# First column group of the second FFN's input projection: two separate projections replaced by one paired group, two of its eight weight pairs by Strassen's scheme

## The chip, the core and the metric

The kernel runs on one core of a Trainium2 chip. The metric is the device time of one launch in microseconds (us). The kernel before was run three times.

## What is computed

The reference is one block of a streaming encoder on 256 frames of width 2048: a feed-forward network (FFN), a mixer with two kinds of attention, cross attention to 256 memory tokens, and a second FFN. Each of the four adds its input times 2^(1/4) and ends in a layer norm. Cut to the part around the change:

```python
def swiglu_ffn(x, w_in, w_out):
    g, u = jnp.split(x @ w_in, 2, axis=-1)
    return (jax.nn.silu(g) * u) @ w_out
...
h = layer_norm(ALPHA * h + xa, ln_x_g[l], ln_x_b[l])
h = layer_norm(ALPHA * h + 0.5 * swiglu_ffn(h, ffn2_w_in[l], ffn2_w_out[l]), ln_ffn2_g[l], ln_ffn2_b[l])
```

Here `x` is 256 x 2048, `w_in` 2048 x 11008 (5504 gate columns, then 5504 up columns) and `w_out` 5504 x 2048, all float32.

## The kernel before

**Numbers.** Every operand of a matmul is kept as two parts, `hi` (the value in the matmul's reduced float32 format) and `lo` (the rest). A product takes three matmuls: x_hi w_hi, x_lo w_hi and x_hi w_lo. A megabyte of weights (128 partitions x 2048 values) is loaded by SyncE (SP) into one of three `raw` tiles; ScalarE (ACT) makes `hi` by two casts of 1024 columns (L264) and VectorE (DVE) makes `lo` by one subtraction (L267). The activations are normalised, turned and split in the same way.

**Tiles.** The contraction of 2048 is 16 steps of 128, called `kt` 0 to 15. The 256 tokens are two halves of 128, `tt` 0 and 1. The activations stand in four tiles T0 to T3 of four `kt` each. A matmul (128 x 128 by 128 x 512) adds into a PSUM bank of 128 tokens x 512 columns; there are eight banks, four named `mm` and four named `at`.

**Column groups.** An FFN's input projection is done in groups of 512 up columns and 512 gate columns. An ordinary group is a *pair group* (`pair_group`, L646): it walks over eight weight pairs, each of two `kt`, 512 up and 512 gate columns, and adds into four banks, one for each token half and each of up and gate. A *plain* pair costs 2 x 2 x 2 x 3 = 24 matmuls (`mm_pair`, L303, matmul at L311). Some pairs are done by Strassen's scheme (`mm_sums`, L347, matmul at L366): the 2 x 2 x 2 block product is made from seven products instead of eight, so 21 matmuls. This needs sums of weight blocks (`weight_sums`: L248 once and L250 twice on DVE, into a tile of 2048 columns, then two casts at L264 into X2 and one subtraction at L267 into X3), sums of activation blocks (`forms_step`, `sum_forms`: L321, four times L325, then a split at L255 and L256), four more banks `qs`, and `shared` (L679 to L684), which turns the four banks into four addends. Where a group has such addends, `hidden` (L716) adds them to the banks (L725, L726) ahead of silu and product.

**The first group of the second FFN** is another kind, `first_group` (L687), since its activations come from the layer norm just ahead of it. It has weight arrays of its own, `ffn2_gate` and `ffn2_up`, of which each megabyte holds four `kt` and 512 columns. Gate comes first: its four loads are all kept, and `skewed` (L813) runs them for token half 0 and then again for token half 1 (`mm_tok`, L298, 12 matmuls a part). Load j reads tile Tj. The kept weights stand in both `hi`/`lo` units and in X0/X1 and H4/H5. Up follows, four loads, each for both halves (24 matmuls a load). In all 8 x 12 + 4 x 24 = 192 matmuls. After each of the last three up loads one `forms_step` is recorded, since the next group needs the forms of pairs 2, 4 and 6.

**The layer norm beside it.** The last part of the cross attention's output projection (`w_xo_r`) is skewed too: token half 0 is finished 48 matmuls before token half 1. In those 48 matmuls DVE finishes the statistics of half 0 (L752, L390, L395), forms 1/sqrt by three Newton steps (L400, L375, then L378 and L379 three times), and the shift `nb` (L403). Then DVE scales quarters 0 and 2 of the row (L413) and ACT quarters 1 and 3 (L415); TensorE (PE) turns each quarter by four transposes against the identity (L421); ACT (L428) and DVE (L430) apply gain and bias, two 128-column blocks each; ACT casts the `hi` part (L255) and DVE subtracts the `lo` part (L256) of tile T0, T1, T2 or T3. The same steps for half 1 are the three pieces `before` that `first_group` weaves into its gate parts.

**What sets the order.** All work is recorded as a list of items with weights (`add`, `weave`); `run` (L179) walks the list, and loads weights ahead of the item that needs them, as far as the two units allow. When it loads an item's weights it also makes the weight sums of the next item in the queue, if that one is a Strassen pair (`form_sums(i + 1)`). A scheduler then puts the instructions of each engine in one fixed order; each engine runs its own list strictly in that order and waits at semaphores.

Of the kernel before, what the change touches and what calls it, by code (L numbers as in the profile page):

```python
# [22 lines left out]
D_FF = 5504  # L23
# [4 lines left out]
SUMS_IN = {2: ("X0", 0), 4: ("X0", 1), 6: None}  # L28
# [13 lines left out]
SUM_HOME = ("X2", "X3"),  # L42
# [59 lines left out]
class Kernel:  # L102
# [197 lines left out]
                        start=(start and j + wi + xi == 0), stop=(stop and j == n - 1 and wi == 1),  # L300
                    )

    def mm_pair(self, ps, w, n, x, kts, first, last):  # L303

        for wi in range(2):
            for j, kt in enumerate(kts):
                for tt in range(2):
                    for g in range(2):
                        c = (2 * j + g) * n
                        for xi in range(2 - wi):  # L310
                            self.last_mm = self.nc.tensor.matmul(  # L311
                                ps[tt, g][:, :n], x.at(xi, kt)[:, tt * P:(tt + 1) * P], w[wi][:, c:c + n],
                                start=first and j + wi + xi == 0, stop=last and j == len(kts) - 1 and wi == 1,
                            )
# [239 lines left out]
    def ffn(self, tag, xT, st, first=None, steps=None, late=None, before=None, tags=None):  # L554
# [6 lines left out]
        for half, nf in enumerate(F_SPLIT):  # L561
# [3 lines left out]
            for g in range(-(-nf // 4)):  # L565
# [118 lines left out]
        nc.vector.tensor_tensor(c, b, q[3], ALU.subtract)  # L684
        qs["add"] = {(0, 0): a, (0, 1): b, (1, 0): u, (1, 1): c}

    def first_group(self, tag, xT, before, ps, fx):  # L687

        t = self.t
        kept = {}  # L690

        def part(tt, g, tags=None, held=0, keep=False, again=False):
            def fn(w=None):
                if keep:
                    kept[g] = w
                w = kept.pop(g) if again else w
                if g == 0:
                    ps[tt, 1] = self.group_tile(0)
                self.mm_tok(ps[tt, 1], tt, w, xT(), range(4 * g, 4 * g + 4), g == 0, g == 3)
            ap = t[tag + "_gate"][0, :, g * 2048:(g + 1) * 2048]  # L700
            self.add(fn, *(() if again else ((ap, tags),)), held=held)

        first = self.collect(lambda: self.skewed(
            part, (), (None, None, ("X0", "X1", "early"), ("H4", "H5"))))
        self.weave(first, dict(zip((0, 3, 4), before)))
        for g in range(4):
            def fn(w, g=g):
                for tt in range(2):
                    if g == 0:
                        ps[tt, 0] = self.group_tile(0)  # L710
                    self.mm_tok(ps[tt, 0], tt, w, xT(), range(4 * g, 4 * g + 4), g == 0, g == 3)
            self.add(fn, t[tag + "_up"][0, :, g * 2048:(g + 1) * 2048])
            if g:
                self.add(self.forms_step(fx, SUMS_IN, tuple(SUMS_IN)[g - 1], xT))

    def hidden(self, ps, j, g, n, hid, qs):  # L716

# [981 lines left out]
def _layout(i):  # L1699
# [8 lines left out]
    for f in ("ffn1", "ffn2"):  # L1708
# [9 lines left out]
    r["ffn2_gate"] = _tok(a["ffn2_w_in"][0][:, :512])  # L1718
    r["ffn2_up"] = _tok(a["ffn2_w_in"][0][:, D_FF:D_FF + 512])
# [57 lines left out]
```

## Time and profile before

| what | value |
|---|---|
| median of three runs | 2434.72 us (2433.43 to 2435.46) |
| the profiled execution's own time | 2432.52 us |
| its span, first to last instruction | 2430.7 us |
| PE busy | 2422.3 us, 11280 matmuls |
| DVE busy | 2130.9 us, 2437 instructions |
| ACT busy | 1553.2 us, 2022 instructions |
| mean granted TensorE clock | 1.000 |

The first group of the second FFN lies at 1742.11 to 1787.54 us from the span's start. In the timeline a row gives start, duration, engine, line, operation, output <- input, shapes and count, and in brackets the idle time ahead of it and what ended that. Rows of one kind are merged, and the duration of a merged row runs from its first start to its last end. The ends of matmuls are modelled and overlap the next start, so starts are compared with starts.

### The profile page before, as it was taken

To read this page: it belongs to the slowest core of one execution; us is meant where nothing else is said; L and a number is where in the kernel's file an instruction comes from. 1 tells how busy PE (TensorE), PEld (TensorE's weight loads), DVE (VectorE), ACT (ScalarE), POOL (GpSimd) and SP (SyncE) were. 2 spreads that over 40 slices of the span, in tenths; PEclk is the share of its full clock that TensorE was granted. 3 is DMA by queue.
4 is the path that set the end of the run, shared out by engine and by line. 5 is a ranking of instruction groups with operands and counts; after the bars stand their busy time and mean duration, and the time that the engine had idled before them with its cause. 6 is when DMAs were issued, how large, how long until landed. Compare 5 with 4: busy or idle time off the path is not lost.

```text
span 2430.7 us, 29702 instructions
## 1 busy us (share of the span) xinstructions
PE 2422.3 (100%) x11280; PEld 2022.8 (83%) x11280; DVE 2130.9 (88%) x2437; ACT 1553.2 (64%) x2022; POOL 35.9 (1%) x81
## 2 busy tenths in 40 slices
PE   9999999999999999999999999999999999999999
PEld 8888888888888888888888888888888888888887
DVE  8999989899889998779788889979879999888997
ACT  6676745666555557878565687765666675556662
POOL 0000000000000001000000000000000000000000
PEclk9999999999999999999999999999999999999999
DMA  7766656667656657776577577655556766666665
GB/s 268 252 212 214 207 200 222 210 201 219 224 176 215 216 195 248 229 210 176 183 246 256 167 241 213 220 181 192 190 199 214 229 221 210 220 207 207 200 220 182
DMA packets 176414, 516.20 MB, mean 212 GB/s; under 512 B 111728, under 2 KB 112496, under 8 KB 121104
## 3 DMA queue, kind: packets, MB, share of 16 engines
q1 hardware_dynamic: 170816, 495.83, 61.6%
q0 software_dynamic: 4592, 17.30, 2.2%
q8 instruction: 88, 1.44, 0.2%
q10 hardware_dynamic: 864, 1.18, 0.1%
q14 instruction: 54, 0.44, 0.1%
HBM read 485.30 MB, written 2.10 MB: 201 GB/s over the span
## 4 chain that ended last, share of the span: by engine, by line
PE 89%; DVE 4%; ACT 3%; DMA 1%; issue 1%; SPq 0%; DVEq 0%; ACTq 0%
PE at L311 24%; PE mm L311 23%; PE at L366 11%; PE mm L366 11%; PE mm L298 10%; PE mm L277 4%; PE mm L279 2%; DVE lo L267 2%; ACT hi L264 1%; PE at L1034 1%; PE at L1505 0%; PE at L277 0%; DMA raw<-w_xv 0%; PE at L1088 0%; ACT H L854 0%
## 5 line engine op out<-in xcount | busy, mean ns | idle before, releaser
L264 ACT CAST hi<-raw 128x1024 fp32r<-128x1024 f32 (+1 forms) x852 | 804.0, 981 | 458.0 <-PE at L311 150.1
L267 DVE TENSOR_TENSOR lo<-raw,hi 128x2048 fp32r<-128x2048 f32 (+1 forms) x427 | 902.0, 2114 | 134.8 <-ACT hi L264 129.0
L311 PE MATMUL mm<-hi,T 128*128 128x512 f32 (+1 forms) x1312 | 307.5, 384 | 0.8 <-DVE v L400 0.7
L311 PEld LDWEIGHTS mm<-hi,T 128*128 128x128 f32 x1312 | 244.5, 188 | 46.9 <-DVE v L400 1.1
L264 ACT CAST X<-H 128x1024 fp32r<-128x1024 f32 (+1 forms) x170 | 174.8, 1035 | 160.9 <-DVE H L248 119.9
L311 PE MATMUL at<-hi,T 128*128 128x512 f32 x1136 | 272.3, 390 | 0.0
L311 PEld LDWEIGHTS at<-hi,T 128*128 128x128 f32 x1136 | 213.3, 188 | 44.5
L267 DVE TENSOR_TENSOR X<-H,X 128x2048 fp32r<-128x2048 f32 (+1 forms) x85 | 191.4, 2252 | 64.7 <-ACT X L264 64.7
L311 PE MATMUL mm<-lo,T 128*128 128x512 f32 (+1 forms) x656 | 158.4, 383 | 0.0
L311 PE MATMUL at<-lo,T 128*128 128x512 f32 x568 | 141.0, 389 | 0.0
L311 PEld LDWEIGHTS mm<-lo,T 128*128 128x128 f32 x656 | 122.3, 188 | 22.4
L311 PE MATMUL at<-hi,H 128*128 128x512 f32 x560 | 133.8, 390 | 0.0
L311 PEld LDWEIGHTS at<-lo,T 128*128 128x128 f32 x568 | 106.7, 188 | 22.1
L311 PEld LDWEIGHTS at<-hi,H 128*128 128x128 f32 x560 | 105.0, 188 | 21.5
L250 DVE TENSOR_TENSOR H<-H,raw 128x512 f32<-128x512 f32 (+1 forms) x170 | 115.4, 679 | 2.2
L311 PE MATMUL mm<-hi,H 128*128 128x512 f32 x480 | 115.5, 392 | 0.1
L311 PEld LDWEIGHTS mm<-hi,H 128*128 128x128 f32 x480 | 89.6, 188 | 18.9 <-DVE w L684 0.5
L248 DVE TENSOR_TENSOR H<-raw 128x1024 f32<-128x1024 f32 (+1 forms) x85 | 102.1, 1201 | 0.6 <-DMA raw<-w_gate 0.4
L366 PE MATMUL mm<-X,X 128*128 128x512 f32 x342 | 91.4, 393 | 0.0
L264 ACT CAST X<-raw 128x1024 fp32r<-128x1024 f32 (+1 forms) x54 | 55.4, 1035 | 47.9 <-DVE raw L250 38.6
L366 PE MATMUL at<-X,X 128*128 128x512 f32 (+1 forms) x315 | 82.6, 386 | 0.7 <-ACT X L264 0.7
L854 ACT COPY w<-w 128x1024 uint16<-128x1024 uint16 (+1 forms) x60 | 75.7, 1275 | 1.4 <-DMA w<-w 1.4
(387 smaller groups left out, 4151.3 us busy)
## 6 DMA issues: line engine op xcount, KB each, us to landing
raw<-ffn_w_in SPq DMA_DIRECT2D x150, 1024.0 KB, 4.9
raw<-ffn_w_out SPq DMA_DIRECT2D x66, 1024.0 KB, 4.9
raw<-w_gate SPq DMA_DIRECT2D x32, 1024.0 KB, 4.8
raw<-ffn_w_out_r SPq DMA_DIRECT2D x16, 1024.0 KB, 4.9
raw<-w_qk SPq DMA_DIRECT2D x16, 1024.0 KB, 5.6
raw<-w_o_b SPq DMA_DIRECT2D x16, 1024.0 KB, 4.8
raw<-w_out SPq DMA_DIRECT2D x16, 1024.0 KB, 5.0
raw<-w_xk SPq DMA_DIRECT2D x16, 1024.0 KB, 5.4
```

Of the source, the lines that this page charges most:

```text
L248: self.nc.vector.tensor_tensor(two[0], two[1], raw[:, :m].unsqueeze(1).to_broadcast([P, 2, m]), ALU.add)
L250: self.nc.vector.tensor_tensor(t[:, a * m:a * m + m], t[:, b * m:b * m + m], raw[:, a * m:a * m + m], ALU.add)
L264: self.last_hi = self.nc.scalar.copy(hi[:, c:d], src[:, c:d])
L267: self.last_lo = self.nc.vector.tensor_tensor(lo[:, :n], src, hi[:, :n].bitcast(F32), ALU.subtract)
L277: self.nc.tensor.matmul(ps, hi[j], x.both(kt), start=(j == 0), stop=False)
L279: self.last_mm = self.nc.tensor.matmul(ps[:, :S], lo[j], x.at(0, kt), start=False, stop=(j == n - 1))
L298: self.last_mm = self.nc.tensor.matmul(ps, x.at(xi, kt)[:, tt * P:(tt + 1) * P], w[wi][:, j * 512 + c:j * 512 + c + m], start=(start and j ...
L311: self.last_mm = self.nc.tensor.matmul(ps[tt, g][:, :n], x.at(xi, kt)[:, tt * P:(tt + 1) * P], w[wi][:, c:c + n], start=first and j + wi + ...
L366: self.last_mm = self.nc.tensor.matmul(bank[:, :m], a[xi], v[wi][:, c * m:(c + 1) * m], start=own and first and wi + xi == 0, stop=own and ...
L854: self.nc.scalar.copy(self.words(u, n).rearrange("p (c k) -> p k c", k=2), self.words(s, n).rearrange("p (k c) -> p k c", k=2))
L1034: nc.tensor.matmul(ps[:, c0:c0 + nk], q[:, tt * P:(tt + 1) * P], k[:, :nk], start=(j == 0), stop=(j == len(parts) - 1))
```

## The change

`first_group` now reads `ffn2_w_in[0]`, laid out in pairs of up and gate as for an ordinary group. Pairs 0 to 3 are run for token half 0 and then, from the kept weights, for token half 1 (`mm_pair` has a new argument for the token halves): 4 x 2 x 12 = 96 matmuls, which read T0 and T1 alone. Then come pair 6 by Strassen's scheme, pair 5 plain, pair 4 by the scheme and pair 7 plain: 21 + 24 + 21 + 24 = 90. That is 186 matmuls in place of 192. The weight sums of pairs 6 and 4 stand in a tile F. The forms of pair 6 are recorded ahead of the last part of token half 1, those of pair 4 after pair 6, and those of pair 2, which only later groups use, after `shared`. The group now has four addends, so `shared` and the longer branch of `hidden` run for it. The arrays `ffn2_gate` and `ffn2_up` are gone. Bytes loaded and the number of loads are the same.

```diff
-    def mm_pair(self, ps, w, n, x, kts, first, last):
+    def mm_pair(self, ps, w, n, x, kts, first, last, tts=(0, 1)):
...
-                for tt in range(2):
+                for tt in tts:
...
-                    main = self.collect(self.first_group, tag, xT, before, ps, fx)
+                    main = self.collect(self.first_group, tag, xT, before, ps, qs, fx)
...
-    def first_group(self, tag, xT, before, ps, fx):
+    def first_group(self, tag, xT, before, ps, qs, fx):
...
-        def part(tt, g, tags=None, held=0, keep=False, again=False):
+        def part(tt, k, tags=None, held=0, keep=False, again=False):
...
-                if g == 0:
-                    ps[tt, 1] = self.group_tile(0)
-                self.mm_tok(ps[tt, 1], tt, w, xT(), range(4 * g, 4 * g + 4), g == 0, g == 3)
-            ap = t[tag + "_gate"][0, :, g * 2048:(g + 1) * 2048]
-            self.add(fn, *(() if again else ((ap, tags),)), held=held)
+                if k == 0:
+                    ps.update({(tt, g): self.group_tile(0) for g in range(2)})
+                self.mm_pair(ps, w, 512, xT(), (2 * k, 2 * k + 1), k == 0, False, (tt,))
+            self.add(fn, *(() if again else ((ap(k), tags),)), held=held)
+
+        def plain(k, last):
+            self.add(lambda w: self.mm_pair(ps, w, 512, xT(), (2 * k, 2 * k + 1), False, last), ap(k))
+
+        def sums(k, first):
+            def fn(w):
+                if first:
+                    qs.update((a, self.group_tile(1)) for a in range(4))
+                self.mm_sums(ps, qs, w, 512, xT(), fx[k], 2 * k, first, not first)
+            self.add(fn, Sums(ap(k), *SUM_HOME, "F"))
 
         first = self.collect(lambda: self.skewed(
             part, (), (None, None, ("X0", "X1", "early"), ("H4", "H5"))))
-        self.weave(first, dict(zip((0, 3, 4), before)))
-        for g in range(4):
...
+        side = dict(zip((0, 3, 4), before))
+        side[7] = [self.forms_step(fx, SUMS_IN, 6, xT, False)]
+        self.weave(first, side)
+        sums(6, True)
+        self.add(self.forms_step(fx, SUMS_IN, 4, xT, False))
+        plain(5, False)
+        sums(4, False)
+        self.add(lambda: self.shared(qs, 512), prio=SOON)
+        self.add(self.forms_step(fx, SUMS_IN, 2, xT, False))
+        plain(7, True)
```

Three places in the instruction order show what moves. All engines' lists are the same up to the first of them, but for the names of the loaded arrays. The first is DVE, in the layer norm of token half 0, from the third Newton step on; `y` and `nb` are 1/sqrt and the shift, `h_101` the row, `T_2159` tile T0. Before:

```order
L378 TENSOR_SCALAR a_13959<-y_13958,v_13957 128x1
L379 TENSOR_SCALAR y_13958<-a_13959,y_13958 128x1
L403 SCALAR_TENSOR_TENSOR nb_13961<-mv_13956,y_13958 128x1
L413 TENSOR_SCALAR h_101<-h_101,mv_13956,y_13958 128x512 x2
L430 TENSOR_SCALAR w_2164_14018<-at_14013,vecs 128x128
L430 TENSOR_SCALAR w_2166_14031<-at_14026,vecs 128x128
L430 TENSOR_SCALAR w_2164_14018<-at_14013,vecs 128x128
L430 TENSOR_SCALAR w_2166_14031<-at_14026,vecs 128x128
L256 TENSOR_TENSOR T_2159_14008<-w_2164_14018,T_2159_14008 128x4x128
```

And now:

```order
L378 TENSOR_SCALAR a_13959<-y_13958,v_13957 128x1
L248 TENSOR_TENSOR F_14102<-raw_14100 128x1024
L379 TENSOR_SCALAR y_13958<-a_13959,y_13958 128x1
L250 TENSOR_TENSOR F_14102<-F_14102,raw_14100 128x512
L403 SCALAR_TENSOR_TENSOR nb_13961<-mv_13956,y_13958 128x1
L413 TENSOR_SCALAR h_101<-h_101,mv_13956,y_13958 128x512 x2
L250 TENSOR_TENSOR F_14102<-F_14102,raw_14100 128x512
L430 TENSOR_SCALAR w_2164_14018<-at_14013,vecs 128x128
```

The three weight sums of pair 6 stand between the Newton step and the last of the operations that the transposes wait for. After these rows, the finish of half 1's row (L752 before, L764 now) and its statistics (L390) also stand ahead of the `lo` part of T0.

The second place is ACT just after it, from the scaling of the row to the cast of T0 (`X_2195` is X2, `T_2159` T0). Before:

```order
L415 ACTIVATE h_101<-h_101,nb_13961,y_13958 128x512 x2
L428 ACTIVATE w_2164_14018<-at_14013,vecs 128x128
L428 ACTIVATE w_2166_14031<-at_14026,vecs 128x128
L428 ACTIVATE w_2164_14018<-at_14013,vecs 128x128
L428 ACTIVATE w_2166_14031<-at_14026,vecs 128x128
L255 CAST T_2159_14008<-w_2164_14018 128x4x128
```

And now:

```order
L415 ACTIVATE h_101<-h_101,nb_13961,y_13958 128x512 x2
L428 ACTIVATE w_2164_14018<-at_14013,vecs 128x128
L428 ACTIVATE w_2166_14031<-at_14026,vecs 128x128
L264 CAST X_2195_14227<-F_14102 128x1024
L428 ACTIVATE w_2164_14018<-at_14013,vecs 128x128
L428 ACTIVATE w_2166_14031<-at_14026,vecs 128x128
L264 CAST X_2195_14227<-F_14102 128x1024
L255 CAST T_2159_14008<-w_2164_14018 128x4x128
```

Two casts of weight sums now stand ahead of the cast of T0.

The third place is DVE in the layer norm of token half 1, from the scaling of its row (`h_102`) on; `H_2178` is the `lo` part of the fourth kept load, `X_2196` is X3. Before:

```order
L413 TENSOR_SCALAR h_102<-h_102,mv_14078,y_14080 128x512 x2
L267 TENSOR_TENSOR H_2178_14096<-raw_14093,H_2177_14095 128x2048
L430 TENSOR_SCALAR w_2181_14143<-at_14138,vecs 128x128
L430 TENSOR_SCALAR w_2183_14156<-at_14151,vecs 128x128
L430 TENSOR_SCALAR w_2181_14143<-at_14138,vecs 128x128
L430 TENSOR_SCALAR w_2183_14156<-at_14151,vecs 128x128
L256 TENSOR_TENSOR T_2159_14008<-w_2181_14143,T_2159_14008 128x4x128
```

And now:

```order
L413 TENSOR_SCALAR h_102<-h_102,mv_14078,y_14080 128x512 x2
L267 TENSOR_TENSOR H_2178_14096<-raw_14093,H_2177_14095 128x2048
L267 TENSOR_TENSOR X_2196_14228<-F_14102,X_2195_14227 128x2048
L430 TENSOR_SCALAR w_2184_14150<-at_14145,vecs 128x128
L430 TENSOR_SCALAR w_2186_14163<-at_14158,vecs 128x128
L430 TENSOR_SCALAR w_2184_14150<-at_14145,vecs 128x128
L430 TENSOR_SCALAR w_2186_14163<-at_14158,vecs 128x128
L256 TENSOR_TENSOR T_2159_14008<-w_2184_14150,T_2159_14008 128x4x128
```

The `lo` part of pair 6's weight sums stands ahead of gain and bias of half 1's first quarters.

More of the change, by code (lines that the diff above doesn't have):

```diff
@@ L685, in shared, with ap @@
         qs["add"] = {(0, 0): a, (0, 1): b, (1, 0): u, (1, 1): c}
-    def first_group(self, tag, xT, before, ps, fx):
-        t = self.t
+    def first_group(self, tag, xT, before, ps, qs, fx):
+        src = self.t[tag + "_w_in"][0]
         kept = {}
-        def part(tt, g, tags=None, held=0, keep=False, again=False):
+        def ap(k):
+            return src[:, k * 2048:(k + 1) * 2048]
+        def part(tt, k, tags=None, held=0, keep=False, again=False):
             def fn(w=None):
                 if keep:
-                    kept[g] = w
-                w = kept.pop(g) if again else w
-                if g == 0:
-                    ps[tt, 1] = self.group_tile(0)
-                self.mm_tok(ps[tt, 1], tt, w, xT(), range(4 * g, 4 * g + 4), g == 0, g == 3)
-            ap = t[tag + "_gate"][0, :, g * 2048:(g + 1) * 2048]
-            self.add(fn, *(() if again else ((ap, tags),)), held=held)
+                    kept[k] = w
+                w = kept.pop(k) if again else w
+                if k == 0:
[10 more added lines that the diff above has]
+            self.add(fn, Sums(ap(k), *SUM_HOME, "F"))
@@ L1717, in _layout @@
         r[f + "_w_out_r"] = _tok(w[F_SPLIT[0] * P:, D // 2:])
-    r["ffn2_gate"] = _tok(a["ffn2_w_in"][0][:, :512])
-    r["ffn2_up"] = _tok(a["ffn2_w_in"][0][:, D_FF:D_FF + 512])
     w = a["w_in"][0]
```

8 lines of the change are left out of this document (removed).

## The prediction, made before the changed kernel was run

> **What bounds the kernel now.** I read the page first, then PE's waits, then the stretch of the changed group by windows, and last the timelines of PE, DVE and ACT there.
>
> ```profile
> span 2430.7 us, 29702 instructions
> PE 2422.3 (100%) x11280; PEld 2022.8 (83%) x11280; DVE 2130.9 (88%) x2437; ACT 1553.2 (64%) x2022; POOL 35.9 (1%) x81
> ```
>
> PE is busy for 2422.3 of 2430.7 us. A matmul taken away is time taken away, unless PE waits in its place. The waits of PE over the whole span are few, and the longest two are these (sum, count, longest):
>
> ```profile
> PE at L493 <- DVE w L470: 1.1, 1, 1.1
> PE at L366 <- ACT X L264: 0.7, 2, 0.5
> ```
>
> So there is hardly a wait to win back. In the stretch of the group PE does not idle at all (the windows row: length, then busy time of PE, PEld, DVE, ACT, POOL, then granted clock):
>
> ```profile
> 1742.00:1788.00 46.00, 46.00 (x215) 38.29 (x213) 34.41 (x63) 25.55 (x41) 0.00 (x0) 1.00 0.35 122
> ```
>
> DVE has 11.6 us free there, so more DVE work fits in the sum; the question is where in the order it stands. PE's timeline gives the fixed points: the transposes of half 0 at 1737.68 and 1741.32, the group's start at 1742.11, the transposes of half 1 at 1750.37, half 1's first gate part at 1754.81, the up loads from 1765.78, and the next group at 1787.54.
>
> ```profile
> 1737.68 1.03 PE L421 MATMUL at<-ident,h 128*128 128x128 f32 x8
> 1738.47 3.00 PE L298 MATMUL mm<-H,X 128*128 128x512 f32 x12
> 1741.32 1.03 PE L421 MATMUL at<-ident,h 128*128 128x128 f32 x8
> 1742.11 2.07 PE L298 MATMUL mm<-hi,T 128*128 128x512 f32 x8
> 1750.37 1.04 PE L421 MATMUL at<-ident,h 128*128 128x128 f32 x8
> 1754.81 2.07 PE L298 MATMUL mm<-hi,T 128*128 128x512 f32 x8
> 1765.78 1.98 PE L298 MATMUL mm<-hi,T 128*128 128x512 f32 x8
> 1787.54 3.79 PE L311 MATMUL at<-hi,T 128*128 128x512 f32 x16
> ```
>
> **The matmuls.** Between 1765.78 and 1787.54 stand the 96 up matmuls: 21.76 / 96 = 0.2267 us each. The change takes 192 - 186 = 6 away: 6 x 0.2267 = 1.36 us. That they do go is seen by counting the rows of the new order, 186. And it is all that can be won: with no wait in the stretch, nothing else can go. The Trainium skill ("TensorE: Matmul & The Clock Gate", Back-to-back issue gap) gives 512 / 2.4 + 2.5 = 216 ns a matmul; by it the six would be worth 1.29 us, and the trace's longer pitch decides.
>
> **The layer norm of half 0.** Here the change puts three weight sums on DVE ahead of the row's scaling. DVE's rows:
>
> ```profile
> 1728.11 2.29 DVE L267 TENSOR_TENSOR lo<-raw,hi 128x2048 fp32r<-128x2048 f32 x1 [2.50 <-ACT hi L264]
> ...
> 1735.93 0.21 DVE L379 TENSOR_SCALAR y<-a,y 128x1 f32<-128x1 f32 x1
> 1736.18 0.16 DVE L403 SCALAR_TENSOR_TENSOR nb<-mv,y 128x1 f32<-128x1 f32 x1
> 1736.26 1.00 DVE L413 TENSOR_SCALAR h<-h,mv,y 128x512 f32<-128x512 f32 x2
> 1738.82 1.78 DVE L430 TENSOR_SCALAR w<-at,vecs 128x128 f32<-128x128 f32 x4 [1.56 <-ACT w L428]
> 1740.86 1.29 DVE L256 TENSOR_TENSOR T<-w,T 128x512 fp32r<-128x512 f32 x2 [0.26 <-ACT T L255]
> 1742.07 0.68 DVE L752 SCALAR_TENSOR_TENSOR h<-h,mm 128x512 f32<-128x512 f32 x1
> 1742.99 0.69 DVE L390 BATCH_NORM_STATS2 bn<-h 128x6 f32<-128x512 f32 x1
> 1743.93 0.25 DVE L395 BATCH_NORM_AGGREGATE mv<-bn 128x2 f32<-128x24 f32 x1
> 1747.82 1.00 DVE L413 TENSOR_SCALAR h<-h,mv,y 128x512 f32<-128x512 f32 x2
> 1753.54 1.29 DVE L256 TENSOR_TENSOR T<-w,T 128x512 fp32r<-128x512 f32 x2 [0.25 <-ACT T L255]
> 1786.24 1.22 DVE L248 TENSOR_TENSOR H<-raw 128x1024 f32<-128x1024 f32 x1
> 1787.49 0.69 DVE L250 TENSOR_TENSOR H<-H,raw 128x512 f32<-128x512 f32 x1
> 1794.93 2.28 DVE L267 TENSOR_TENSOR X<-H,X 128x2048 fp32r<-128x2048 f32 x1
> ```
>
> A row that does not need the one ahead of it starts about 0.08 us before that one's end (1736.18 + 0.16 against 1736.26), so L248 takes 1.14 and L250 0.61 of DVE's time. The load that L248 needs is issued when the `lo` row of 1728.11 is done:
>
> ```profile
> 1730.43 32.17 SPq L193 DMA_DIRECT2D raw<-ffn_up  x4
> DMA to landing us min/median/max: 4.6/4.9/6.1
> ```
>
> It lands at 1730.43 + 4.9 = 1735.3; DVE comes to L248 at 1735.93, so it waits for no load (with the longest landing, 6.1, it waits 0.6). The order now is L248, L379, L250, `nb`, L413: the scaling starts at 1735.93 + 1.14 + 0.14 (L379) + 0.61 + 0.08 (`nb`) = 1737.90 in place of 1736.26, 1.64 late. Half of the 1.00 us later, at some 1738.44, quarter 0 is scaled. PE reaches the transposes at 1737.68 as before and starts at 1738.48: a wait of 0.80 us. The margin there was 1737.68 less 1736.8, some 0.9 us, and the change asks for 1.64.
>
> PE then does 12 matmuls and eight transposes and is at the group at 1742.11 + 0.80 = 1742.91. T0 is late by more, since ACT has two new casts. ACT's rows:
>
> ```profile
> 1736.38 1.52 ACT L415 ACTIVATE h<-h,nb,y 128x512 f32<-128x512 f32 x2 [1.93 <-DVE nb L403]
> 1738.32 1.83 ACT L428 ACTIVATE w<-at,vecs 128x128 f32<-128x128 f32 x4 [0.42 <-PE at L421]
> 1740.20 1.14 ACT L255 CAST T<-w 128x512 fp32r<-128x512 f32 x2
> 1751.01 1.83 ACT L428 ACTIVATE w<-at,vecs 128x128 f32<-128x128 f32 x4 [1.55 <-PE at L421]
> 1790.63 1.05 ACT L264 CAST X<-H 128x1024 fp32r<-128x1024 f32 x1
> ```
>
> L415 moves with `nb` to 1738.02 and ends at 1739.54; the 0.42 us that ACT idled ahead of L428 are used up. Two L428 end at 1740.4, the first cast (1.05) at 1741.4, two more L428 at 1742.2, the second cast at 1743.2, and the cast of T0 at 1743.7. DVE meanwhile does L752 and L390 for half 1, whose matmuls end at 1742.1, and is free at 1743.9; the `lo` part of T0 (0.69) ends at 1744.62. PE does two matmuls on the `hi` part while it waits. So it loses 1744.65 - 0.45 - 1742.91 = 1.29 us.
>
> **The layer norm of half 1.** From 1744.62 on DVE has the steps that took it from 1743.93 (the second statistics) to its scaling at 1747.82, 3.9 us, and between them T1's `lo` part and one L430 row that stood earlier before, 1.1 us: the scaling of half 1 starts at about 1749.7 and ends at 1750.7. PE comes to half 1's transposes at 1750.37 + 2.09 = 1752.46, so nothing waits there; the late start has given this norm more time. Then the kept load's `lo` part (2.29) runs to 1753.0 and the new X3 row (2.28) to 1755.2. ACT's first L428 starts 0.64 us after the transposes, as 1751.01 is after 1750.37, and ends at 1753.6, so DVE is 1.6 us late for gain and bias. Four of them alternate with ACT's (1.8 us), the casts and `lo` follow as at 1753.54, and T0 of half 1 is whole at 1757.9. PE wants its third matmul on it at 1754.81 + 2.09 + 0.45 = 1757.35: a wait of 0.55 us. The range is 0 to 1.7, since T0's `lo` part was done 0.6 us ahead of its use before (1753.54 + 0.69 against 1754.81) and the new row is 2.28.
>
> **After that.** Half 1's 48 matmuls give DVE 10.9 us to make what pair 6 needs. The prices of the small rows, with one row on the slack that this stretch had (count, sum, mean, idle time ahead):
>
> ```profile
> L267 DVE TENSOR_TENSOR lo<-raw,hi 128x2048 fp32r<-128x2048 f32 x5 | 11.4, 2291 | 9.5 <-ACT hi L264 9.5
> L321 DVE TENSOR_TENSOR w<-T 128x512 f32<-128x512 f32 x3 | 2.1, 685 | 0.0
> L325 DVE TENSOR_TENSOR w<-w,w 128x128 f32<-128x128 f32 x6 | 1.7, 287 | 0.0
> ```
>
> I count from 1757.9: four L430 and three L256 rows (4 x 0.45 + 3 x 0.65 = 3.7), three weight sums of pair 4 (2.3), the `lo` parts of pair 6 (1536 columns, three quarters of 2.29, 1.7) and of pair 5 (2.3), and of the forms two L321 and six small rows (1.3 + 6 x 0.25 = 2.8): 12.8 us, up to 1770.7. The form that PE needs first is done some 0.4 earlier, at 1770.3; PE wants it for its tenth matmul of the pair, at 1757.5 + 57 x 0.2267 = 1770.4. No wait, or up to 0.5 us. From there 80 matmuls (18.1 us) are left, against 13.6 us of DVE rows: the rest of the forms of pair 4 (1.4), four `lo` parts (1.7 + 3 x 2.2), and `shared` with a weight sum (4 x 0.61 + 1.14). That is 4 us of slack, where the group before idled 9.5 us ahead of its `lo` rows, and I take nothing for it. The four additions of `hidden` (4 x 0.61) come behind the group, where PE is on other banks. The transfers that turn the hidden tile go out later, but their result is wanted only by the output projection, after the half's five other groups. Loads are the same in number and size.
>
> **The sum.** -1.36 + 0.80 + 1.29 + 0.55 = +1.28 us. The profiled execution took 2432.52 (span 2430.7, 1.8 around it), so its like after the change takes 2433.8. It lay 2.2 below the median of the runs, 2434.72, and the forecast for the median is 2434.72 + 1.3 = 2436.0. Ends of the waits: 1.4 in sum (each step 0.4 better than I count) and 4.5 (the longest landing, +0.6; half 1 at 1.7, and pair 6 at 0.5), so +0.0 to +3.1, 2434.7 to 2437.8. About 0.2%, 4.9 us, is what a measurement of this kernel tells from no change.
>
> **Rivals.**
>
> *The gain alone.* The norm has more cover than I count, PE waits nowhere, and 1.36 us go: 2433.4. For it: T0 to T1 are all that the first 48 matmuls read now, so quarters 2 and 3 are no longer urgent. Against it: the quarters that count are the first ones, and the margin at the first transposes (0.9) is less than the 1.64 us put ahead. Chance 0.08.
>
> *The new rows are paid in full (the other side).* At the norms of both halves PE would wait for all that stands ahead: 2.6 (L248 and two L250) + 2.1 (two casts) on half 0 and 2.3 (X3) on half 1, with nothing hidden behind PE's 12 matmuls. 7.0 - 1.36 = +5.6: 2440.3, slower by over 0.2%. It decides from a sum of waits of 4.9 + 1.36 = 6.3 us on. For it: DVE, ACT and PE hand each other every quarter of the row, so a delay on one can be a delay on all. Against it: one of the L250 stands behind the scaling, and ACT idled 0.42 us. Chance 0.08.
>
> *The clock falls.* The tail of the kernel shows a granted clock under full once PE stops. Windows of the last 8 us:
>
> ```profile
> 2423.00:2427.00 4.00, 3.28 (x8) 1.14 (x6) 3.60 (x10) 0.61 (x2) 1.27 (x1) 1.00 0.18 66
> 2427.00:2431.00 4.00, 0.00 (x0) 0.00 (x0) 0.66 (x2) 0.00 (x0) 0.00 (x0) 0.76 0.55 197
> ```
>
> PE's work ends 3.28 us into the first. A mean of 0.76 in the second is, if the clock fell to half, 1.9 us at half, begun 2.8 us after PE stopped. If my two waits at half 0 were one of that length, some matmuls after it would run slow; 4 us at 0.76 lose 1.0 us, twice that is 2: 2437 to 2438. Against it: the waits are 0.8 and 1.3 us, with 12 matmuls between. Chance 0.05. The Trainium skill ("TensorE: Matmul & The Clock Gate", Why this matters for your kernels) warns of idle gaps over about 3 us between bursts of matmuls; by that rule, too, my waits are too short, and the tail agrees.
>
> Faster by over 0.2% would need 4.9 us of waits that PE does not have: 0.03, for what I don't see.
>
> **Numbers.** Forecast 0.76, the gain alone 0.08, paid in full 0.08, the clock 0.05, unseen gains 0.03. Same: 0.76 + 0.08 + 0.05 = 0.89; slower 0.08; faster 0.03. The range reaches from the gain alone less the runs' spread below the median (2433.4 - 1.3 = 2432.1) to the forecast's upper end and the clock's, with the spread above (2437.8 + 0.7 = 2438.5, and 2438), say 2438.8; it leaves out the last rival and the unseen.
>
> **What would show it.** Right: PE waits at L421 for `h` (0.8) and at L311 for T0 twice (1.3 and 0.5), and the stretch from 1737.68 to the next group is about 51.1 in place of 49.86 us. Wrong: no wait at L421; a wait for F's load; waits of over 5 us in sum; or waits anywhere in the pairs after half 1.

## The result and the profile after

| | before | after |
|---|---|---|
| median of 22 runs each, us | 2433.93 | 2437.60 |
| lowest to highest, us | 2432.65 to 2437.57 | 2436.05 to 2439.78 |
| profiled execution, us | 2432.52 | 2436.78 |

The ratio is 1.0015, 95% interval 1.0008 to 1.0021: the changed kernel is 3.7 us slower, between 2.0 and 5.1. The forecast was +1.3 us, 2436.0, range 2432.1 to 2438.8, and "within 0.2%" with a chance of 0.89. The sign and the range held; most of the time was lost at a place that the prediction had priced at nothing.

The head of the page of the changed kernel:

```profile
span 2435.0 us, 29705 instructions
PE 2423.3 (100%) x11274; PEld 2019.5 (83%) x11274; DVE 2143.3 (88%) x2453; ACT 1557.3 (64%) x2028; POOL 35.9 (1%) x81
```

Six matmuls are gone, 16 DVE and 6 ACT instructions have come, and PE is still busy all the time. PE's waits from 1735 us on (sum, count, longest):

```profile
PE mm L366 <- ACT X L264: 0.6, 1, 0.6
PE mm L311 <- DVE w L684: 0.4, 2, 0.2
PE mm L311 <- DVE T L256: 0.3, 1, 0.3
PE at L421 <- DVE h L413: 0.2, 1, 0.2
PE at L366 <- ACT X L264: 0.2, 1, 0.2
PE mm L311 <- ACT T L255: 0.2, 1, 0.2
PE at L311 <- DVE w L684: 0.2, 1, 0.2
```

The waits at L421 and for T0 are those foretold, and the fifth row is a wait that the kernel before has too (0.5 us there). The three at L684 and the first row are new and were not foretold: L684 is the last row of `shared`, and the changed group never waits for it. PE's timeline gives the places, from the 12 matmuls ahead of the first transposes to PE's last row:

```profile
1736.16 2.88 PE L298 MATMUL mm<-H,X 128*128 128x512 f32 x12
1739.25 1.09 PE L421 MATMUL at<-ident,h 128*128 128x128 f32 x8 [0.20 <-DVE h L413]
...
1744.13 0.73 PE L311 MATMUL mm<-hi,T 128*128 128x512 f32 x2 [0.16 <-ACT T L255]
1745.20 1.65 PE L311 MATMUL mm<-hi,T 128*128 128x512 f32 x6 [0.33 <-DVE T L256]
...
1757.48 2.14 PE L311 MATMUL mm<-hi,T 128*128 128x512 f32 x8
...
1788.96 3.33 PE L311 MATMUL at<-hi,T 128*128 128x512 f32 x14
...
2429.22 1.02 PE L1629 MATMUL mm<-T,w 128*128 128x512 f32 x2
```

Before, the same two ends were (the next group's start, 1787.54, stands in the prediction):

```profile
1734.96 2.89 PE L298 MATMUL mm<-H,X 128*128 128x512 f32 x12
...
2425.26 1.02 PE L1617 MATMUL mm<-T,w 128*128 128x512 f32 x2
```

So the difference of 4.0 us between the two profiled executions has three parts. *Ahead of the change* PE is 1736.16 - 1734.96 = 1.20 us late, although the lists are the same there. *From these 12 matmuls to the next group* it is 52.80 in place of 52.58 us: +0.22. *From there to the end* it is 640.26 in place of 637.72: +2.54, in groups that the change does not touch. The experiments are read by these three numbers, taken from the same rows of each profile:

| kernel | start of the 12 | to the next group | from there to the end | median, us | runs |
|---|---|---|---|---|---|
| before | 1734.96 | 52.58 | 637.72 | 2433.93 | 22 |
| after | 1736.16 | 52.80 | 640.26 | 2437.60 | 22 |
| e1_plain | 1734.97 | 52.60 | 637.77 | 2434.05 | 11 |
| e2_arrays | 1735.95 | 53.29 | 640.95 | 2437.80 | 11 |
| e3_late_sums | 1736.61 | 53.25 | 641.67 | 2439.45 | 11 |
| e4_dve_load | 1736.13 | 52.58 | 637.98 | 2434.30 | 11 |
| e5_turn_late | 1736.84 | 52.53 | 637.61 | 2433.77 | 11 |
| e6_sums_behind | 1735.81 | 51.82 | 640.71 | 2436.40 | 11 |
| e7_both | 1736.08 | 51.75 | 637.60 | 2432.90 | 11 |
| e8_order_in_before | 1736.44 | 52.58 | 642.51 | 2437.72 | 12 |
| e9_both_again | 1734.81 | 51.79 | 637.97 | 2432.31 | 11 |
| e10_turn_late_before | 1735.70 | 52.58 | 638.09 | 2434.27 | 11 |
| e11_casts_behind | 1736.06 | 51.69 | 640.29 | 2435.61 | 1 |

Where an expectation speaks of 638.3 us for the last stretch, it counts from one matmul earlier to the very last one, 0.66 us more.

**The later groups.** In the kernel after, DVE's rows in the third ordinary group after the changed one, up to the last of `shared` (L681 to L684):

```profile
1906.09 2.29 DVE L267 TENSOR_TENSOR X<-H,X 128x2048 fp32r<-128x2048 f32 x1
1908.29 0.69 DVE L256 TENSOR_TENSOR H<-w,H 128x512 fp32r<-128x512 f32 x1
1909.74 0.69 DVE L256 TENSOR_TENSOR H<-w,H 128x512 fp32r<-128x512 f32 x1 [0.76 <-ACT H L255]
1910.35 0.68 DVE L681 TENSOR_TENSOR w<-w,mm 128x512 f32<-128x512 f32 x1
1911.13 0.69 DVE L682 TENSOR_TENSOR w<-w,w 128x512 f32<-128x512 f32 x1
1911.74 2.29 DVE L267 TENSOR_TENSOR lo<-raw,hi 128x2048 fp32r<-128x2048 f32 x1
1913.94 0.68 DVE L683 TENSOR_TENSOR w<-w,mm 128x512 f32<-128x512 f32 x1
1914.54 0.68 DVE L684 TENSOR_TENSOR w<-w,mm 128x512 f32<-128x512 f32 x1
```

The same place before:

```profile
1904.79 2.28 DVE L267 TENSOR_TENSOR lo<-raw,hi 128x2048 fp32r<-128x2048 f32 x1
1906.99 0.68 DVE L681 TENSOR_TENSOR w<-w,mm 128x512 f32<-128x512 f32 x1
1907.59 0.68 DVE L256 TENSOR_TENSOR H<-w,H 128x512 fp32r<-128x512 f32 x1
...
1908.80 0.68 DVE L256 TENSOR_TENSOR H<-w,H 128x512 fp32r<-128x512 f32 x1
1909.40 0.68 DVE L683 TENSOR_TENSOR w<-w,mm 128x512 f32<-128x512 f32 x1
1909.99 0.68 DVE L684 TENSOR_TENSOR w<-w,mm 128x512 f32<-128x512 f32 x1
1910.59 2.28 DVE L267 TENSOR_TENSOR lo<-raw,hi 128x2048 fp32r<-128x2048 f32 x1
```

The rows are the same, their order is not. `H<-w,H` is the `lo` part of the turned hidden tile of the group before. It stood between the rows of `shared`; now both halves stand ahead of `shared`, and for the second one DVE waits 0.76 us for ACT. A `lo` row of 2.29 us stood behind `shared` (1910.59); now the row of that load stands inside (1911.74). In both kernels it is the 344th row `lo<-raw,hi` from the start, and the row at 1904.79 is the 343rd, which now stands at 1903.88. L684 frees the fourth bank for the next group, whose seventh matmul wants it. In the kernel before L684 ended at 1910.67, 1.38 us ahead of that group's start at 1912.05. Now it ends at 1915.22, 1.67 us behind the start at 1913.55. Of these 3.05 us the `lo` row makes 2.20 and the wait for ACT 0.76. The seventh matmul is due 6 x 0.2267 = 1.36 us behind the start, at 1914.91, and waits. The four later waits in PE's timeline of the kernel after:

```profile
1915.28 2.11 PE L311 MATMUL mm<-hi,T 128*128 128x512 f32 x8 [0.20 <-DVE w L684]
1958.10 1.89 PE L311 MATMUL at<-hi,T 128*128 128x512 f32 x7 [0.16 <-DVE w L684]
1971.50 0.73 PE L366 MATMUL mm<-X,X 128*128 128x512 f32 x2 [0.64 <-ACT X L264]
2001.16 1.88 PE L311 MATMUL mm<-hi,H 128*128 128x512 f32 x7 [0.15 <-DVE w L684]
```

Counted from start to start, with the matmul behind each that is late as well, the three at L684 cost 1.33 us and the one at X 0.91 us: 2.24 of the 2.54.

The third of these rows comes from ACT's order. After, the cast that it waits for stands behind a cast of the next load, which waits for that load's transfer:

```profile
1969.45 1.06 ACT L264 CAST hi<-raw 128x1024 fp32r<-128x1024 f32 x1 [0.99 <-DMA raw<-ffn_w_in]
1970.41 1.04 ACT L264 CAST X<-H 128x1024 fp32r<-128x1024 f32 x1
```

Before, it stood ahead of it:

```profile
1965.39 1.06 ACT L264 CAST X<-H 128x1024 fp32r<-128x1024 f32 x1 [0.51 <-DVE H L250]
1967.57 1.57 ACT L264 CAST hi<-raw 128x1024 fp32r<-128x1024 f32 x2 [1.12 <-DMA raw<-ffn_w_in]
```

The Trainium skill ("PSUM — Partial Sum Buffer", Engine vs sequencer instructions) says that the queues of ScalarE and VectorE are strictly first in, first out. These rows agree: L683, which needs nothing of the `lo` row, starts when that row is done.

### The profile page after: what moved, and what is told of

It reads as the page before. It is cut to its first block, busy times and chain, and to the rows that moved or that the text cites. A ratio compares the mean times of both kernels' runs of the same rounds, so it can differ in the third digit from the quotient of the medians.

```text
span 2435.0 us, 29705 instructions
## 1 busy us (share of the span) xinstructions
PE 2423.3 (100%) x11274; PEld 2019.5 (83%) x11274; DVE 2143.3 (88%) x2453; ACT 1557.3 (64%) x2028; POOL 35.9 (1%) x81
## 4 chain that ended last, share of the span: by engine, by line
PE 86%; DVE 6%; ACT 4%; DMA 2%; issue 2%; SPq 0%; DVEq 0%; ACTq 0%
PE mm L311 24%; PE at L311 23%; PE at L366 11%; PE mm L366 10%; PE mm L298 7%; PE mm L277 4%; DVE lo L267 3%; PE mm L279 2%; ACT hi L264 2%; PE at L1046 1%; DMA raw<-ffn_w_in 1%; DVE X L267 0%; DMA raw<-w_xq 0%; DMA raw<-w_xv 0%; PE at L1517 0%
## 5 line engine op out<-in xcount | busy, mean ns | idle before, releaser
L311 PE MATMUL mm<-hi,T 128*128 128x512 f32 (+1 forms) x1376 | 323.6, 384 | 2.2 <-DVE v L400 1.2
L311 PEld LDWEIGHTS mm<-hi,T 128*128 128x128 f32 x1376 | 255.8, 188 | 51.9 <-DVE v L400 1.6
L311 PE MATMUL mm<-lo,T 128*128 128x512 f32 (+1 forms) x688 | 166.6, 383 | 0.0
L311 PEld LDWEIGHTS mm<-lo,T 128*128 128x128 f32 x688 | 128.2, 188 | 23.7
L366 PE MATMUL mm<-X,X 128*128 128x512 f32 x342 | 91.5, 392 | 0.6 <-ACT X L264 0.6
L366 PE MATMUL at<-X,X 128*128 128x512 f32 (+1 forms) x324 | 85.0, 386 | 0.4 <-ACT X L264 0.4
L366 PEld LDWEIGHTS mm<-X,X 128*128 128x128 f32 x342 | 63.5, 188 | 16.1 <-DVE X L267 1.7
```

The costliest lines, as they stand in the source:

```text
L311: self.last_mm = self.nc.tensor.matmul(ps[tt, g][:, :n], x.at(xi, kt)[:, tt * P:(tt + 1) * P], w[wi][:, c:c + n], start=first and j + wi + ...
L366: self.last_mm = self.nc.tensor.matmul(bank[:, :m], a[xi], v[wi][:, c * m:(c + 1) * m], start=own and first and wi + xi == 0, stop=own and ...
```

## The experiments

Three theories were open. *Lag*: the added DVE work (12.4 us in all) makes DVE late, and it carries the lag into groups where it has little idle time. *Order*: the scheduler wrote the later groups' rows in another order, and that order makes PE wait. *Memory*: two arrays are gone, so that the others lie elsewhere, and loads land otherwise.

**e1_plain.** The Strassen pairs of the changed group are made plain, and its weights laid out for that.

```diff
-        side[7] = [self.forms_step(fx, SUMS_IN, 6, xT, False)]
...
-        sums(6, True)
-        self.add(self.forms_step(fx, SUMS_IN, 4, xT, False))
+        plain(4, False)
         plain(5, False)
-        sums(4, False)
-        self.add(lambda: self.shared(qs, 512), prio=SOON)
-        self.add(self.forms_step(fx, SUMS_IN, 2, xT, False))
+        self.add(self.forms_step(fx, SUMS_IN, 2, xT))
+        plain(6, False)
+        self.add(self.forms_step(fx, SUMS_IN, 4, xT))
         plain(7, True)
+        self.add(self.forms_step(fx, SUMS_IN, 6, xT))
...
```

> The group keeps the new pair order, its array and its four kept pairs, but all eight pairs are plain: 192 matmuls, no weight sums, no shared, no longer branch of hidden. Strassen's extra DVE work as the cause (local and later waits): the three waits at the layer norms (0.36, 0.44 and 0.61 us of PE's time, the second matmul's included) and the L684 waits in the later groups go, and the stretch from 1734.96 us to the next group is 52.6 to 52.9 us. Pair order as the cause: the waits stay. Arrays gone as the cause of the 1.2 us ahead of the group: PE comes to the 12 matmuls ahead of the first transposes at 1736.2 as in the changed kernel, and the time is 2434 + 1.2 = 2435.2; else at 1735.0, and the time is 2434 to 2434.5.

2434.05 us, ratio 0.9998 (0.9990 to 1.0007), stretches 52.60 and 637.77: the kernel before again, without a wait from 1735 us to the end but the one for X that the kernel before has too. The pair order, the new array and the kept loads cost nothing; all that was lost belongs to the two Strassen pairs.

**e2_arrays.** The changed kernel with the two unused arrays among its inputs.

```diff
+    r["ffn2_gate"] = _tok(a["ffn2_w_in"][0][:, :512])
+    r["ffn2_up"] = _tok(a["ffn2_w_in"][0][:, D_FF:D_FF + 512])
```

> The changed kernel with the two unused arrays ffn2_gate and ffn2_up kept among its inputs; no instruction differs. Arrays gone (another placement in memory) as the cause of the 1.2 us that PE is late ahead of the group: that falls to 0.3 or less, and the time is about 2436.4. Run-to-run spread or a fixed property of the changed instructions as the cause: the time stays at 2437.0 to 2438.0, and where PE stands at the 12 matmuls ahead of the first transposes varies between 1734.9 and 1736.3 with no system.

2437.80 us, ratio 1.0016 (1.0007 to 1.0025), as the changed kernel, and PE at 1735.95. The memory theory falls. The lists ahead of the 12 matmuls are the same in all thirteen kernels, and these start anywhere from 1734.81 to 1736.84: the 1.20 us is spread between executions.

**e3_late_sums.** The last four pairs in the order plain 5, Strassen 6, plain 7, Strassen 4 (with the flags that close the banks moved along).

```diff
...
+        plain(5, False)
         sums(6, True)
         self.add(self.forms_step(fx, SUMS_IN, 4, xT, False))
-        plain(5, False)
+        plain(7, True)
         sums(4, False)
         self.add(lambda: self.shared(qs, 512), prio=SOON)
         self.add(self.forms_step(fx, SUMS_IN, 2, xT, False))
-        plain(7, True)
```

> The changed kernel with the last four pairs in the order plain 5, Strassen 6, plain 7, Strassen 4, so that the weight sums of pair 6 are made after the kept loads and not in the layer norm of half 0. 186 matmuls as in the changed kernel. Weight sums in the layer norm as the cause of the waits there: no wait at L421 and at L311 for T0 (1.3 to 1.5 us less by 1788 us). Carried DVE lag as the cause of the later waits: the L684 waits stay or grow, since the same DVE work is done later, and the time is 2436 to 2437. Reordered rows in the later groups as the cause: the waits stay at the same places with the same size, since their order is the same as in the changed kernel, 2436.1.

2439.45 us, ratio 1.0022 (1.0013 to 1.0031): worse, and not a clean test. Weight sums are made when the load ahead of theirs is handled, and that was still in the layer norm of half 0. The first sum now stood behind the scaling of the row, but waited 1.60 us for its load, and the casts ahead of T0's waited for the sum. The wait at L421 went and that for T0 grew to 1.3 us.

**e4_dve_load.** The kernel before with 20 additions that nothing reads, five after each up load.

```diff
+            self.add(self.more)
...
+    def more(self):
+        v = self.w2()
+        for _ in range(5):
+            self.nc.vector.tensor_tensor(v, self.h[0][:, :512], self.h[0][:, 512:1024], ALU.add)
```

> The kernel before with 20 additions of 128 x 512 on DVE that nothing reads (about 0.61 us each, 12.2 us) among the four up loads of the first group; every later row and all of PE's list are as before. Carried lag (DVE enters the next groups late and stays late): PE waits at L684 or at X in the third to sixth group after it, 1 to 3 us in sum, and the time is 2435 to 2437. Reordered rows in the later groups as the cause: their order is the old one here, so no such wait, and the time is 2434 to 2434.3; a wait inside the first group itself (up to 2 us) is seen by its place.

2434.30 us, ratio 1.0001 (0.9992 to 1.0010), 637.98 us, no wait at L684. That the lag was there and went is seen in DVE's rows of the next ordinary group. Before (the group starts at 1787.54):

```profile
1809.47 4.08 DVE L267 TENSOR_TENSOR lo<-raw,hi 128x2048 fp32r<-128x2048 f32 x2
...
1820.12 2.29 DVE L267 TENSOR_TENSOR lo<-raw,hi 128x2048 fp32r<-128x2048 f32 x1 [1.13 <-ACT hi L264]
```

With the additions (the group starts at 1788.71):

```profile
1813.13 3.95 DVE L267 TENSOR_TENSOR lo<-raw,hi 128x2048 fp32r<-128x2048 f32 x2
...
1821.28 2.29 DVE L267 TENSOR_TENSOR lo<-raw,hi 128x2048 fp32r<-128x2048 f32 x1 [0.79 <-ACT hi L264]
```

At the first row DVE is 24.42 us behind the group's start in place of 21.93, 2.5 late; at the second 32.57 in place of 32.58. A lag of 2.5 us is gone within one group. In the changed kernel the row of the second load is

```profile
1821.14 2.28 DVE L267 TENSOR_TENSOR lo<-raw,hi 128x2048 fp32r<-128x2048 f32 x1
```

It starts 32.18 us behind its group's start (1788.96), so DVE is not late there, and the first wait at L684 is 94 us further on. The lag theory falls; e5 below, with all of the change's DVE work in place, has no such wait either.

**e5_turn_late.** The changed kernel; the split of the turned hidden tile is recorded after `shared`.

```diff
...
+                    self.second = True
...
-                    turn[5] = turn.pop(6)
+                    turn[5] = turn.pop(8 if self.second else 6)
...
-        return product, {2: [send], 6: [turn]}
+        return product, {2: [send], 8 if self.second else 6: [turn]}
```

> The changed kernel with one thing recorded later: in the second FFN's groups the turned hidden tile of the group before is split (L255, L256) after shared instead of ahead of pair 6, so that in the three groups with L684 waits the two L256 rows stand between the rows of shared, as in the kernel before. The first group and the layer norms are as in the changed kernel. Order of DVE's rows as the cause of the later waits: shared's last row (L684) ends 0.7 us or more earlier against PE, the three L684 waits (0.43 us each with the second matmul) go, and the time falls by 1.3 to 2436.3. Lag carried from the first group as the cause: the waits stay, 2437.6.

2433.77 us, ratio to before 0.9999 (0.9990 to 1.0008), last stretch 637.61: all that the later groups had lost came back, 2.65 us, more than the 1.3 expected, since the wait for X went too (that cast again stands ahead of the one that waits for a transfer). DVE's rows at the same place (lines are 1 or 2 higher):

```profile
1908.86 2.29 DVE L268 TENSOR_TENSOR lo<-raw,hi 128x2048 fp32r<-128x2048 f32 x1
1911.07 0.68 DVE L683 TENSOR_TENSOR w<-w,mm 128x512 f32<-128x512 f32 x1
1911.66 0.69 DVE L257 TENSOR_TENSOR H<-w,H 128x512 fp32r<-128x512 f32 x1
...
1914.07 0.68 DVE L686 TENSOR_TENSOR w<-w,mm 128x512 f32<-128x512 f32 x1
```

The splits stand inside `shared` again, as in the kernel before, and the wait for ACT is gone; the `lo` row, now at 1908.86, still stands ahead. PE's fourth bank is free at 1914.75, 0.81 us behind the group's start at 1913.94, and the seventh matmul, due at 1913.94 + 1.36 = 1915.30, does not wait.

**e6_sums_behind.** The changed kernel; pair 6's weight sums queued behind L403, their split behind the cast of T1.

```diff
...
+                with self.tc.issue_after(self.chain.ins) if home == "F" else nullcontext():
+                    sums[i] = self.weight_sums(raw, queue[i].m, self.block(home, (P, 2048)) if home else self.raw_tile())
...
+                with self.tc.issue_after(self.ln_act.ins) if w.stage == "F" else nullcontext():
+                    got = got[0], self.halves(sums[i][:, :n], *(self.block(g, (P, 2048), F32R) for g in w.tags))
```

> The changed kernel with the weight sums of pair 6 queued on DVE behind the 1/sqrt and shift (L403) last recorded, and their split queued on ACT behind the cast of T1 last recorded; both move out of the layer norm of half 0. The later groups' order stays that of the changed kernel. Weight sums and casts in the layer norm as the cause of the waits at L421 and L311: the 0.36, 0.44 and 0.61 us there go (1.4 us less by 1788 us), the later waits stay, and the time is 2436.2. If the later place is too late for pair 6, a wait of up to 2 us stands at L366 near 1771 us instead and nothing is won.

2436.40 us, ratio 1.0008 (1.0000 to 1.0017). The three waits at the norm are gone, and the stretch falls from 52.80 to 51.82 us; 0.4 us comes back at L366: at pair 6 and at pair 4 two matmuls each start 0.1 us late. The later groups still lose 640.71 - 637.72 = 3.0 us.

**e7_both and e9_both_again.** Both edits together, on two chips.

> Both of the last two edits together. If the waits at the layer norm and the L684 waits are what ate the gain, the time is 2437.6 - 1.4 - 1.3 = 2434.9, and if the wait for X in the later groups (0.9 us) goes with the new order too, 2434.0; the full gain of the six matmuls would be 2432.7. If the lost time sits elsewhere, it stays above 2436.5.

> The kernel with both edits (the split of the turned hidden tile behind shared, the weight sums of pair 6 behind the layer norm of half 0) once more, on another chip beside the next one. From the stretches of its first profile against the kernel before (0.8 us less from the 12 matmuls ahead of the transposes to the next group, 0.1 less after it) it gains 0.95 us: 2433.1 where the kernel before takes 2434.1. If its 2432.9 was spread, 2434 or more.

2432.90 us, ratio 0.9995 (0.9986 to 1.0003), and 2432.31 us, ratio 0.9996 (0.9987 to 1.0005). Stretches 51.75 and 637.60, 51.79 and 637.97. The medians lie 1.2 and 1.6 us under that of the kernel before on the same chip, where the stretches give 0.95 and 0.54; each interval still holds "no change". This is the version nearest to the full gain of 1.36 us; that it is faster than the kernel before is not shown.

**e8_order_in_before.** The kernel before; in the second FFN `shared`'s first DVE row is queued behind the last split of the turned hidden tile.

```diff
...
-        nc.vector.tensor_tensor(u, a, q[2], ALU.add)
+        with self.tc.issue_after(self.turn_lo.ins) if in_group and self.turn_lo is not None else nullcontext():
+            nc.vector.tensor_tensor(u, a, q[2], ALU.add)
...
+            self.turn_lo = self.split_lo
```

> The kernel before, first group untouched, with shared's first DVE row in the second FFN's later groups queued behind the two L256 rows of the turned hidden tile: the order that the changed kernel has in its three waiting groups. No row is added or removed. Order as the cause of the later waits: PE waits at L684 in those groups, 0.3 to 0.5 us each, and the time rises by 0.9 to 1.5 us to 2435.0 to 2435.6. Added DVE work or lag as the cause: no such waits, 2434.1.

2437.72 us, ratio 1.0013 (1.0004 to 1.0021), last stretch 642.51: no row added, no matmul taken away, and 4.8 us more in the profile. PE's longest waits from 1735 us on:

```profile
PE at L367 <- ACT X L265: 1.2, 1, 1.2
PE at L367 <- DVE X L268: 0.8, 1, 0.8
PE mm L367 <- ACT X L265: 0.8, 1, 0.8
```

Order alone can cost that much. What was expected wrongly is where: two of the waits at L684 are there, but small (PE starts 0.31 and 0.20 us late), and most of the loss is at X, since the scheduler moved rows of ACT along; the first row is the kernel before's own wait of 0.5 us, grown. So the run shows what an order of the lists can cost, not what this one row costs. That the order costs the changed kernel its 2.5 us is shown by e5.

**e10_turn_late_before.** The edit of e5 in the kernel before.

> The kernel before with the split of the turned hidden tile recorded behind shared in the second FFN, first group untouched. If that edit only takes away waits that the change made, nothing is there to win: 2434.1, and the stretch after the group stays at 638.3 to 638.4 us. If the edit is a gain of its own, which the change merely shares, the stretch falls below 637.5 us and the time below 2433.3; then the changed first group is worth nothing beside it.

2434.27 us, ratio 1.0001 (0.9992 to 1.0010), last stretch 638.09. The edit is no gain of its own.

**e11_casts_behind.** Of e6, only the second line: the sums stay on DVE where they are, and only their split is queued behind the cast of T1.

> The changed kernel with only the two casts of pair 6's weight sums (ACT, into X2) queued behind the cast of T1; the three weight sums stay where they are on DVE. By the prediction's split of the waits, the sums cause the wait at L421 (0.36 us in the changed kernel) and the casts the two waits for T0 (1.03 us): the first stays, the other two go, and the stretch to the next group falls by 0.9 to 1.0 us from the changed kernel's. If the sums on DVE alone hold the whole chain, all three waits stay. The later groups' order and waits are those of the changed kernel.

One run, 2435.61 us, stretch 51.69. ACT at the norm and PE after it:

```profile
1739.81 1.72 ACT L429 ACTIVATE w<-at,vecs 128x128 f32<-128x128 f32 x4
1741.66 1.14 ACT L256 CAST T<-w 128x512 fp32r<-128x512 f32 x2
```

```profile
1742.54 1.04 PE L422 MATMUL at<-ident,h 128*128 128x128 f32 x8
1743.34 2.09 PE L312 MATMUL mm<-hi,T 128*128 128x512 f32 x8
```

T0's cast follows gain and bias at once, and PE goes from the transposes to the group in 0.80 us as before, eight matmuls in a row: with the two casts moved, the wait for T0 is gone. The scheduler also put T0's first `lo` row ahead of half 1's row again (L764 and L390 in the changed kernel), so the run does not separate the casts from these two rows in the 0.62 us that PE waited for the `lo` part. At L421 PE starts only 0.07 us late here, against what was expected. That does not clear the sums: with the same lists of DVE and PE up to there PE started 0.37, 0.82 and 0.07 us late in the changed kernel, in e2 and in e5.

## Why the prediction was right or wrong

**The matmuls: right.** Six are gone, and nothing speaks for more than their 1.36 us: the two stretches of e7 and e9 are together 0.95 and 0.54 us shorter than those of the kernel before.

**L421, 0.80 us: right in kind; the size is not fixed.** It was 0.37, 0.82, 0.07 and 0.07 us in the changed kernel, e2, e5 and e11, with the same lists of DVE and PE up to there. What counts is how far DVE lies behind PE. Its first scaling row starts 2.49, 2.94, 2.19 and 2.20 us after the first of PE's 12 matmuls in these four profiles, and 0.70 to 1.41 us after it in the nine whose kernels have no sums ahead of that row. So the sums do delay the row; but the number was worked out from one execution, in which the distance was 1.30 (1736.26 - 1734.96), and e2 happens to have just its 1.30 + 1.64.

**T0 of half 0, 1.29 us: right in kind, a little too large.** In the changed kernel PE starts 0.41 late on the `hi` part and 0.62 on the `lo` part, 1.03; in e2 and e5 1.02 as well. e11 shows the two casts as the cause, together with the two DVE rows that went along with them.

**T0 of half 1, 0.55 us: wrong; under 0.1 us was waited.** T0 was whole when it was counted to be, by 1757.9:

```profile
1757.21 0.69 DVE L256 TENSOR_TENSOR T<-w,T 128x512 fp32r<-128x512 f32 x1 [0.34 <-ACT T L255]
```

But PE, 1.2 us late from ahead of the group, wanted it at 1757.48 + 0.45 = 1757.93 and not at 1757.35. Its first eight matmuls there take 1.98 us from start to start, in place of 1.90.

**Pair 6, none: right.** Its 21 matmuls take from 1768.52 to the next pair's start at 1773.32, 0.2286 us each.

**The group as a whole, +1.28 us: too much.** Measured +0.22, and +0.71 and -0.05 in e2 and e5; the 51.1 us that were to show it right came out as 52.80 - 2.72 = 50.08.

**After that, nothing: this step failed.** The prediction's sum has no term for what comes behind the group, and it said of the hidden tile's transfers that "their result is wanted only by the output projection". As a matter of data that is so. But the rows that split the turned tile have come to stand in DVE's list ahead of `shared`, and a `lo` row inside it, and DVE starts its rows in the order of its list, as the rows above show. So they hold up `shared`, whose banks the next group wants. The orders compared were those at the group and the norm. From the next group to where the lists agree again DVE has some 250 rows and ACT some 210, and about 40 and 30 of them stand elsewhere than before, as do about 20 of PE's matmuls; none of them was priced. They cost 2.54 us (3.23 in e2). e5 takes that away. It isn't the number of moved rows: e5's lists differ from those of the kernel before in twice as many, and lose nothing. What counts is what has come to stand ahead of the last rows of `shared` and of the cast into X. The prediction did name waits in the pairs after half 1 as what would prove it wrong; there are such waits, but in groups whose order it had not compared.

**The range held by luck.** Its upper end stood for long waits at the norm. These came out shorter than the forecast, and most of the 3.7 us is the term that the sum does not have. With the later order mended and the norm as it is (e5), the median is 2433.77, which is no change, and not 2436.0. Two sums are off besides, and decide nothing: the upper ends of the waits as they are listed add up to 0.80 + 0.6 + 1.29 + 1.7 + 0.5 = 4.9 us and not 4.5, and DVE's rows behind pair 6's forms to 13.3 us and not 13.6.

**The rivals.** The waits "paid in full" are not it: at the norm they sum to 1.4 us, not 7.0. The clock neither. The granted clock (third figure from the end) in the changed group and in all that follows, by windows:

```profile
1744.00:1789.00 45.00, 44.54 (x203) 36.57 (x204) 39.34 (x65) 25.60 (x43) 0.00 (x0) 1.00 0.39 139
1789.00:2429.00 640.00, 638.61 (x2849) 529.83 (x2848) 579.98 (x573) 393.23 (x453) 5.56 (x9) 1.00 0.63 210
```

It stays at 1.00. The Trainium skill ("TensorE: Matmul & The Clock Gate", Why this matters for your kernels) warns of idle gaps over about 3 us; the longest new wait of the changed kernel is 0.64 us, and the trace agrees, though no run here comes near that length.

**What stays open.** Why the scheduler turned the later rows round when the group's work changed is not shown; e1 and e4 only show that neither the new pair order nor more DVE work does it. The lists of DVE, ACT and PE changed together in every run that changed the later order, so the share of each engine's order is not separated. The stretches of the profiles explain +2.76 (after) and +3.94 us (e2) of the medians' 3.7; which part of the rest is spread can't be said.

## What to carry to other kernels

Where a scheduler writes the lists, an edit reaches as far as the lists differ, and not as far as its data go: compare the order to the place where it agrees again, and price every row that has moved ahead of a row that frees a buffer. A wait worked out from one execution holds for one phase of the engines; give it a range from the spread of that phase. And before an edit that saves little is given up, look where the time went: here two edits of order took back 4.7 to 5.3 us of median, more than the edit had cost.

## What the runs showed beside that

A wait costs PE more than the list of waits says. At 1915.28 the list gives 0.20 us of idle time, since the modelled end of the matmul ahead overlaps it; start to start PE is 0.37 us late, and the next matmul follows after 0.335 in place of 0.227 us, 0.11 late again. That second step, 0.10 to 0.115 us, stands behind each wait for DVE or ACT that the timelines of the thirteen profiles show from 1735 us on at matmuls of 512 or 384 columns; at the two such waits of the transposes it is 0.06. So the three waits at L684, 0.6 us in the list, cost 1.3. And the same lists, up to 1735 us, ended 2.0 us apart in thirteen profiles, more than the whole gain of the six matmuls.
